# Two-layer streaming encoder on one core: the three cheap steps of each up-projection block moved from places 2, 4 and 5 to places 1, 3 and 5

## The chip, the cores and the metric

The kernel runs on one core of a Trainium2 chip. The metric is the device time of one execution in microseconds (us), lower being better. Three runs of the kernel before are shown, and one further execution was recorded by the profiler.

In the profile, PE is the matrix engine's matmuls and PEld its weight loads, DVE is the vector engine, ACT the scalar engine, POOL the GpSimd engine, and SP the engine whose queue issues the loads.

## The reference, cut to what matters

The input is 256 tokens of width 2048. Two layers each mix tokens in three groups of attention heads, project back, and then apply a multilayer perceptron (MLP) with 8192 hidden columns. All numbers are float32. The part that the change touches is the second line of the MLP:

```
h = rms_norm(x, mlp_norm[l])
u = h @ w_up[l]                      # (256 x 2048) @ (2048 x 8192)
x = x + square(relu(u)) @ w_down[l]  # (256 x 8192) @ (8192 x 2048)
```

## The kernel before, in words

**Blocks.** In each layer the MLP walks over four quarters of the hidden columns (`qt`). A quarter is two up-projection blocks and then two down-projection blocks, each one an instance of `Product`. In names a block is `u` or `d`, the quarter, and 0 or 1: `u10` and `u11` are the up blocks of quarter 1, and `u?0` below stands for the first block of any quarter. There are 16 up blocks and 16 down blocks. A block multiplies 256 rows by 1024 columns and sums over eight *steps* `i` = 0 to 7 of 256 each (line 321, `step`). Weights of a step are two halves of 128x1024, 512 KB each.

**A float32 product from three matmuls.** A weight half arrives in a `raw` tile. ACT copies its head into `wh` (line 154) and DVE subtracts to get the rest, `wl` (line 155). The activations were split in the same way. Each block product is then three matmuls, head by head, head by rest and rest by head (line 313, `add`).

**Plain steps and steps with sums.** A step is a 2x2 by 2x2 product of blocks. A plain step does all eight block products, 24 matmuls of 512 columns. The steps in a list (`S_UP` for up blocks, `S_DOWN` for down blocks, line 278) do it with seven block products of sums and differences, 21 matmuls. For that, DVE forms four combinations of the weights in place (lines 345 to 348), ACT and DVE split those into `th` and `tl`, and the combinations of the activations (`sums`) are made once per layer, while the output projection's results are added to x (lines 801 to 803). In such a step the matmuls come in the order p1, p2, p3 (nine matmuls from `wh` and `wl`), p5, p7, p6, p4 (twelve from `th` and `tl`).

**Buffers.** `raw` has 4 buffers and `wh` and `wl` have 5 each, in all of the kernel. A step with sums loads its halves into `rs`, of which there are 3, and its combinations go to `th` and `tl`, of which there are 2 each. A step with sums takes two of the three `rs` buffers: half 0 holds b11 and b21, half 1 holds b12 and b22. `th_2`/`tl_2` are made from half 1 and come first, `th_3`/`tl_3` from half 0. After `tl_2` half 1's buffer is free, after `tl_3` half 0's.

**What hangs on a block's end.** At the last step with sums (place 5 before and after the change, line 361) DVE begins to combine the accumulators (lines 365 to 369), and at the block's end it adds the rest (line 375). An up block's result gets its ReLU on ACT (line 819), is turned by transposes on PE (line 384), squared on ACT and split on ACT and DVE (`hidden`, four calls). These four calls wait in a list, and `more()` takes one after each pair of block products of a plain step, so all four run in step 0 of the block that follows.

**Order.** A scheduler puts the instructions of each engine into one fixed order when the kernel is built; each engine runs its own list in that order, and waits for others by semaphores. All the weight loads are issued from SP's list, so that a load that waits for a free buffer holds up the loads that stand behind it.

Of the kernel before, what the change touches and what calls it, by code (L numbers as in the profile page):

```python
# [36 lines left out]
def hybrid_encoder(ctx: ExitStack, tc: tile.TileContext, xT, wA, wQ, wKV, wB, wC, wO, wU, wD,  # L37
# [237 lines left out]

    S_UP, S_DOWN = (2, 4, 5), (2, 5)
    HALF = (slice(0, P), slice(P, T))

    later = []
# [688 lines left out]
def build(shapes):  # L970
    import concourse.bacc as bacc

    nc = bacc.Bacc("TRN2", target_bir_lowering=False, num_devices=1)
    args = [nc.dram_tensor(f"in_{n}_dram", shapes[n], F32, kind="ExternalInput").ap() for n in _ORDER]
    args.append(nc.dram_tensor("out_0_dram", (T, D), F32, kind="ExternalOutput").ap())
    with tile.TileContext(nc) as tc:
        hybrid_encoder(tc, *args)
    return nc
# [9 lines left out]
```

## Time and profile before

| | us |
|---|---|
| median of 3 runs (lowest, highest) | 2089.03 (2084.41, 2090.4) |
| the profiled execution, and its span | 2083.71, 2081.9 |
| DVE busy | 1710.9 (82%) |
| ACT busy | 1191.1 (57%) |
| POOL busy | 184.1 (9%) |
| PE busy | 2030.8 (98%) |

Busy time is the time in which an engine executed instructions. PE's clock was granted nearly in full (0.994 on average over the span). The second quarter of the first layer's MLP, as an example, has its two up blocks from 507.44 to 595.60 us of the span and its two down blocks from there to 682.15 us. An engine other than PE matters here only where PE stood and waited for it.

### The profile page before, as it was taken

The numbers are of one execution on the slowest core, as the hardware profiler recorded it, in microseconds if no ns is written. First come the engines' busy times: TensorE is split into PE (matmuls) and PEld (weight loads), VectorE is DVE, ScalarE is ACT, GpSimd is POOL, SyncE is SP. The second block draws the span as 40 slices with busy tenths as digits, with TensorE's granted clock in tenths as the row PEclk, the third lists the DMA queues.
The fourth block names the chain that finished last, engine by engine and source line by source line (L and its number), as shares of the span: only waits on it lengthen the run. The fifth ranks groups of instructions, "written<-read, shape, count | busy, mean of one in ns | idle before, by whom it ended". The sixth has DMA issues, their size and how long they took to land.

```text
span 2081.9 us, 27549 instructions
## 1 busy us (share of the span) xinstructions
PE 2030.8 (98%) x9984; PEld 1694.1 (81%) x9984; DVE 1710.9 (82%) x2427; ACT 1191.1 (57%) x1721; POOL 184.1 (9%) x241
## 2 busy tenths in 40 slices
PE   8999999999999999999999999999999999999997
PEld 6888888888778778878788888877887787787886
DVE  7766697888888888789976766978888988988986
ACT  6666655554664565465566666546546645645663
POOL 5101141000000000000231012400000000000000
PEclk9999999999999999999999999999999999999999
DMA  7534454555556546556445345545555555465562
GB/s 255 191 125 173 148 201 160 189 207 183 181 193 221 188 167 205 180 179 216 161 160 180 130 157 177 194 173 186 179 189 181 205 210 172 172 212 199 195 212 92
DMA packets 106840, 379.92 MB, mean 182 GB/s; under 512 B 11984, under 2 KB 13392, under 8 KB 106704
## 3 DMA queue, kind: packets, MB, share of 16 engines
q1 hardware_dynamic: 104976, 374.85, 51.8%
q10 hardware_dynamic: 1296, 1.62, 0.3%
q8 instruction: 78, 1.28, 0.2%
q0 software_dynamic: 432, 1.70, 0.2%
q14 instruction: 58, 0.48, 0.1%
HBM read 376.03 MB, written 2.10 MB: 182 GB/s over the span
## 4 chain that ended last, share of the span: by engine, by line
PE 68%; DVE 13%; DMA 9%; issue 5%; ACT 4%; POOL 1%; SPq 0%; ACTq 0%; POOLq 0%; DVEq 0%
PE p_d L313 23%; PE p_u L313 8%; PE e_d L313 6%; DMA rs_u<-in_wU_dram 6%; PE ps_wo L164 4%; DVE wl_u L155 3%; DVE tl_u L155 3%; PE ps_wo L165 2%; ACT wh_u L154 2%; PE e_u L313 2%; PE ps_qC L164 1%; PE ps_kC L164 1%; PE ps_kB L164 1%; PE ps_qB L164 1%; DMA raw_d<-in_wD_dram 1%
## 5 line engine op out<-in xcount | busy, mean ns | idle before, releaser
L313 PE MATMUL p_d<-wh_d,h_u 128*128 128x512 f32 x1280 | 420.6, 392 | 0.0
L313 PE MATMUL p_u<-wh_u,xm 128*128 128x512 f32 x1152 | 386.7, 394 | 0.0
L154 ACT CAST wh_d<-raw_d 128x1024 fp32r<-128x1024 f32 x192 | 201.0, 1053 | 195.1 <-PE e_d L313 61.7
L313 PEld LDWEIGHTS p_d<-wh_d,h_u 128*128 128x128 f32 x1280 | 240.1, 188 | 49.4
L313 PEld LDWEIGHTS p_u<-wh_u,xm 128*128 128x128 f32 x1152 | 218.1, 189 | 45.5
L155 DVE TENSOR_TENSOR wl_d<-raw_d,wh_d 128x1024 fp32r<-128x1024 f32 x192 | 232.7, 1221 | 24.5 <-ACT wh_d L154 23.9
L313 PE MATMUL p_d<-wl_d,h_u 128*128 128x512 f32 x640 | 249.4, 390 | 0.0
L154 ACT CAST wh_u<-raw_u 128x1024 fp32r<-128x1024 f32 x160 | 164.8, 1049 | 120.0 <-PE p_u L313 49.4
L313 PE MATMUL p_u<-wl_u,xm 128*128 128x512 f32 x576 | 226.1, 392 | 0.0
L155 DVE TENSOR_TENSOR wl_u<-raw_u,wh_u 128x1024 fp32r<-128x1024 f32 x160 | 193.0, 1218 | 11.5 <-ACT wh_u L154 10.6
L154 ACT CAST wh_u<-rs_u 128x1024 fp32r<-128x1024 f32 x96 | 80.4, 837 | 138.6 <-DMA rs_u<-in_wU_dram 82.4
L155 DVE TENSOR_TENSOR wl_u<-rs_u,wh_u 128x1024 fp32r<-128x1024 f32 x96 | 90.9, 956 | 71.5 <-ACT wh_u L154 70.0
L313 PEld LDWEIGHTS p_d<-wl_d,h_u 128*128 128x128 f32 x640 | 120.5, 188 | 24.3
L313 PE MATMUL e_d<-wh_d,h_u 128*128 128x512 f32 x384 | 134.7, 391 | 0.0
L154 ACT CAST th_u<-rs_u 128x1024 fp32r<-128x1024 f32 x96 | 100.1, 1049 | 49.1 <-DVE rs_u L348 24.2
L313 PEld LDWEIGHTS p_u<-wl_u,xm 128*128 128x128 f32 x576 | 109.4, 190 | 22.3
L155 DVE TENSOR_TENSOR tl_u<-rs_u,th_u 128x1024 fp32r<-128x1024 f32 x96 | 116.4, 1218 | 10.0 <-ACT th_u L154 9.5
L313 PE MATMUL p_u<-th_u,s_xm 128*128 128x512 f32 x288 | 103.1, 403 | 13.7 <-ACT th_u L154 13.7
L313 PE MATMUL e_u<-wh_u,xm 128*128 128x512 f32 x320 | 112.4, 392 | 0.0
L155 DVE TENSOR_TENSOR wl_d<-rs_d,wh_d 128x1024 fp32r<-128x1024 f32 x64 | 62.7, 980 | 52.0 <-ACT wh_d L154 52.0
L154 ACT CAST wh_d<-rs_d 128x1024 fp32r<-128x1024 f32 x64 | 53.4, 834 | 91.0 <-PE p_d L313 71.4
L140 DVE TENSOR_TENSOR wl_wo<-raw_wo,wh_wo 128x1024 fp32r<-128x1024 f32 x64 | 85.4, 1335 | 20.1 <-ACT wh_wo L139 19.6
(464 smaller groups left out, 4766.1 us busy)
## 6 DMA issues: line engine op xcount, KB each, us to landing
raw_d<-in_wD_dram SPq DMA_DIRECT2D x192, 512.0 KB, 5.2
raw_u<-in_wU_dram SPq DMA_DIRECT2D x160, 512.0 KB, 4.6
rs_u<-in_wU_dram SPq DMA_DIRECT2D x96, 512.0 KB, 4.0
raw_wo<-in_wO_dram SPq DMA_DIRECT2D x64, 512.0 KB, 3.7
rs_d<-in_wD_dram SPq DMA_DIRECT2D x64, 512.0 KB, 4.8
raw_qB<-in_wB_dram SPq DMA_DIRECT2D x16, 512.0 KB, 4.3
raw_kB<-in_wB_dram SPq DMA_DIRECT2D x16, 512.0 KB, 4.0
raw_vB<-in_wB_dram SPq DMA_DIRECT2D x16, 512.0 KB, 4.3
```

What stands on the lines that cost most here:

```text
L140: nc.vector.tensor_tensor(wl[:, :n], raw[:, :n], as32(wh[:, :n]), op=ALU.subtract)
L154: nc.scalar.copy(h, src)
L155: (eng or nc.vector).tensor_tensor(l, src, as32(h), op=ALU.subtract)
L164: nc.tensor.matmul(ps, wh, a, start=i == 0, stop=False)
L165: nc.tensor.matmul(ps[:, 1, :], wl, a[:, 0, :], start=False, stop=i == n - 1)
L313: nc.tensor.matmul(self.ps[b], x, y, start=self.n[b] == 1, stop=self.n[b] == self.total[b])
```

## The change

One table of places is changed. Step 5 keeps its sums; the sums of step 2 go to step 1 and those of step 4 go to step 3. The number of plain steps and of steps with sums stays the same in every block, and so does every operation's count and size. The down blocks are not changed.

```
-    S_UP, S_DOWN = (2, 4, 5), (2, 5)
+    S_UP, S_DOWN = (1, 3, 5), (2, 5)
```

What the scheduler makes of it is seen at three places. Names have the block, the layer, the step and the half or combination: `rs_u10_0_5_1` is block u10 in layer 0, step 5, half 1.

The first is SP's list of loads for block u10. Before:

```order
L328 DMA raw_u10_0_6_0_5425<-in_wU_dram 128x1024
L328 DMA raw_u10_0_6_1_5426<-in_wU_dram 128x1024
L328 DMA raw_u10_0_7_0_5461<-in_wU_dram 128x1024
L328 DMA rs_u10_0_4_1_5329<-in_wU_dram 128x1024
L328 DMA rs_u10_0_5_0_5373<-in_wU_dram 128x1024
L328 DMA raw_u10_0_7_1_5462<-in_wU_dram 128x1024
L328 DMA rs_u10_0_5_1_5374<-in_wU_dram 128x1024
```

The same place in SP's list after the change:

```order
L328 DMA raw_u10_0_6_0_5425<-in_wU_dram 128x1024
L328 DMA rs_u10_0_3_1_5293<-in_wU_dram 128x1024
L328 DMA raw_u10_0_6_1_5426<-in_wU_dram 128x1024
L328 DMA rs_u10_0_5_0_5373<-in_wU_dram 128x1024
L328 DMA raw_u10_0_7_0_5461<-in_wU_dram 128x1024
L328 DMA rs_u10_0_5_1_5374<-in_wU_dram 128x1024
```

The second half of the middle step with sums now stands two loads earlier, and the second half of step 5 has a plain step's time more between it and the one before.

The second place is DVE's list at the start of block u11, where the four `hidden` calls of u10 run (`h0` to `h3` and `sf_h2` are theirs, and line 375 ends u10). Before, from the last line 375 on:

```order
L375 TENSOR_TENSOR c1_u10_0_5419<-e_u10_0_5200,c1_u10_0_5419 128x512
L155 TENSOR_TENSOR wl_u11_0_2_0_5634<-rs_u11_0_2_0_5629,wh_u11_0_2_0_5633 128x1024
L155 TENSOR_TENSOR h0_u10_0_5527<-a0_u10_0_5525,h0_u10_0_5527 128x2x256
L155 TENSOR_TENSOR wl_u11_0_2_1_5645<-rs_u11_0_2_1_5630,wh_u11_0_2_1_5644 128x512
L345 TENSOR_TENSOR rs_u11_0_2_1_5630<-rs_u11_0_2_1_5630 128x512
L155 TENSOR_TENSOR h1_u10_0_5544<-a1_u10_0_5542,h1_u10_0_5544 128x2x256
L346 TENSOR_TENSOR rs_u11_0_2_1_5630<-rs_u11_0_2_0_5629,rs_u11_0_2_1_5630 128x512
```

After:

```order
L375 TENSOR_TENSOR c1_u10_0_5419<-e_u10_0_5200,c1_u10_0_5419 128x512
L346 TENSOR_TENSOR rs_u11_0_1_1_5594<-rs_u11_0_1_0_5593,rs_u11_0_1_1_5594 128x512
L155 TENSOR_TENSOR wl_u11_0_2_0_5647<-raw_u11_0_2_0_5642,wh_u11_0_2_0_5646 128x1024
L347 TENSOR_TENSOR rs_u11_0_1_0_5593<-rs_u11_0_1_1_5594,rs_u11_0_1_0_5593 128x512
L155 TENSOR_TENSOR tl_u11_0_1_2_5620<-rs_u11_0_1_1_5594,th_u11_0_1_2_5619 128x1024
L155 TENSOR_TENSOR h0_u10_0_5527<-a0_u10_0_5525,h0_u10_0_5527 128x2x256
L348 TENSOR_TENSOR rs_u11_0_1_0_5593<-rs_u11_0_1_0_5593 128x512
L155 TENSOR_TENSOR wl_u11_0_2_1_5663<-raw_u11_0_2_1_5643,wh_u11_0_2_1_5662 128x1024
L155 TENSOR_TENSOR h1_u10_0_5544<-a1_u10_0_5542,h1_u10_0_5544 128x2x256
L293 TENSOR_TENSOR sf_h2_u10_0_5568<-a2_u10_0_5563 128x128 x2
L293 TENSOR_TENSOR sf_h2_u10_0_5568<-sf_h2_u10_0_5568,a2_u10_0_5563 128x128
L155 TENSOR_TENSOR tl_u11_0_1_3_5632<-rs_u11_0_1_0_5593,th_u11_0_1_3_5631 128x1024
```

The first step with sums of u11 is now prepared among the work that the end of u10 leaves, and its `tl` come ahead of `h2` and `h3`. Behind these rows DVE's list goes on with h2, one sf, wl of step 3's halves, s_h2, h3, line 345 of step 3, wl of step 4's half 0, lines 346 to 348, wl of step 4's half 1, and then step 3's two `tl`.

The third place is DVE's list at the start of the first layer's MLP (line 781 adds the output projection's last result to x, in two parts). After the change:

```order
L345 TENSOR_TENSOR rs_u00_0_1_1_3778<-rs_u00_0_1_1_3778 128x512
L346 TENSOR_TENSOR rs_u00_0_1_1_3778<-rs_u00_0_1_0_3777,rs_u00_0_1_1_3778 128x512
L347 TENSOR_TENSOR rs_u00_0_1_0_3777<-rs_u00_0_1_1_3778,rs_u00_0_1_0_3777 128x512
L781 TENSOR_TENSOR x7_in_80<-ps_wo15_0_3671,x7_in_80 128x256
L348 TENSOR_TENSOR rs_u00_0_1_0_3777<-rs_u00_0_1_0_3777 128x512
L781 TENSOR_TENSOR x7_in_80<-ps_wo15_0_3671,x7_in_80 128x256
```

Before, the two parts of line 781 stood together, ahead of all four combinations.

## Rows read from the trace of the kernel before

**Rows 1.** The page's first section: busy us (share of the span) xinstructions.

```profile
span 2081.9 us, 27549 instructions
PE 2030.8 (98%) x9984; PEld 1694.1 (81%) x9984; DVE 1710.9 (82%) x2427; ACT 1191.1 (57%) x1721; POOL 184.1 (9%) x241
```

**Rows 2.** Waits of PE: who waited for whom, us in total, times, longest us.

```profile
PE p_u L313 <- ACT th_u L154: 13.7, 16, 1.6
PE p_u L313 <- DVE tl_u L155: 6.9, 8, 1.2
```

**Rows 3.** Timeline of PE, block u10: start, us, what, count, [idle before <-releaser].

```profile
530.79 0.39 PE L313 MATMUL p_u<-tl_u,s_xm 128*128 128x512 f32 x1
...
535.10 0.39 PE L313 MATMUL p_u<-wh_u,s_xm 128*128 128x512 f32 x1
536.16 0.73 PE L313 MATMUL p_u<-th_u,s_xm 128*128 128x512 f32 x2 [0.68 <-ACT th_u L154]
536.73 0.40 PE L313 MATMUL p_u<-wh_u,xm 128*128 128x512 f32 x1
537.88 0.50 PE L313 MATMUL p_u<-tl_u,s_xm 128*128 128x512 f32 x1 [0.75 <-DVE tl_u L155]
538.21 0.39 PE L313 MATMUL p_u<-th_u,s_xm 128*128 128x512 f32 x1
```

**Rows 4.** The chain that ended last, 500 to 600 us: start us, us, what.

```profile
516.91 4.79 DMA rs_u<-in_wU_dram
...
527.50 3.56 DMA rs_u<-in_wU_dram
```

**Rows 5.** Timeline of DVE, block u10.

```profile
515.66 2.35 DVE L155 TENSOR_TENSOR tl_u<-rs_u,th_u 128x1024 fp32r<-128x1024 f32 x2
...
526.26 1.22 DVE L155 TENSOR_TENSOR tl_u<-rs_u,th_u 128x1024 fp32r<-128x1024 f32 x1
...
536.61 1.21 DVE L155 TENSOR_TENSOR tl_u<-rs_u,th_u 128x1024 fp32r<-128x1024 f32 x1
```

**Rows 6.** Timeline of ACT, end of block d01 (the cast is u10's, step 2, half 0).

```profile
507.64 1.06 ACT L154 CAST wh_u<-rs_u 128x1024 fp32r<-128x1024 f32 x1 [1.66 <-PE e_d L313]
```

**Rows 7.** Timeline of PE: u11's first matmuls and step 5, last up block's step 5.

```profile
550.96 0.39 PE L313 MATMUL p_u<-wh_u,xm 128*128 128x512 f32 x1
...
552.32 0.60 PE L384 MATMUL t_u<-ident,c_u 128*128 128x128 f32 x4
552.67 0.48 PE L313 MATMUL p_u<-wh_u,xm 128*128 128x512 f32 x1
552.99 0.40 PE L313 MATMUL p_u<-wl_u,xm 128*128 128x512 f32 x1
...
582.01 0.73 PE L313 MATMUL p_u<-th_u,s_xm 128*128 128x512 f32 x2 [0.68 <-ACT th_u L154]
...
1969.29 0.73 PE L313 MATMUL p_u<-th_u,s_xm 128*128 128x512 f32 x2 [0.52 <-ACT th_u L154]
```

**Rows 8.** Timeline of DVE, block u11, from the last line 375 of u10 on.

```profile
551.31 0.68 DVE L375 TENSOR_TENSOR c_u<-e_u,c_u 128x512 f32<-128x512 f32 x1
552.28 1.23 DVE L155 TENSOR_TENSOR wl_u<-rs_u,wh_u 128x1024 fp32r<-128x1024 f32 x1 [0.30 <-ACT wh_u L154]
554.65 0.69 DVE L155 TENSOR_TENSOR h_u<-a_u,h_u 128x512 fp32r<-128x512 f32 x1 [1.15 <-ACT h_u L154]
...
557.19 0.68 DVE L346 TENSOR_TENSOR rs_u<-rs_u,rs_u 128x512 f32<-128x512 f32 x1
557.79 0.48 DVE L293 TENSOR_TENSOR sf_h_u<-a_u 128x128 f32<-128x128 f32 x2
558.20 0.68 DVE L155 TENSOR_TENSOR h_u<-a_u,h_u 128x512 fp32r<-128x512 f32 x1
```

**Rows 9.** Busy us (x instructions) of each engine in blocks u10 and u11.

```profile
507.44:551.30 43.86, 42.43 (x186) 34.49 (x185) 37.39 (x43) 23.05 (x26) 0.00 (x0) 1.00 0.53 187
551.30:595.60 44.30, 43.62 (x199) 35.33 (x198) 39.07 (x51) 28.55 (x36) 0.00 (x0) 1.00 0.53 185
```

## The prediction, made before the changed kernel was run

> **What bounds the kernel now.** I read the page's head first. PE is busy for 2030.8 of 2081.9 us [rows 1], so the change can only earn what PE loses in waiting. The view of PE's waits says where that is: 16 waits for `th_u` and 8 for `tl_u`, 20.6 us in all [rows 2], every one of them in an up block. In PE's timeline all 24 stand in step 5, the second of the two neighbouring steps with sums. A first block of a quarter (u?0) has two, as in [rows 3]; a second block (u?1) has one of 0.52 to 0.68 us, the 0.68 in u11 and the 0.52 in the last of the eight [rows 7]. The eight of u?1 add to 4.8 us, so the sixteen of u?0 hold 15.8.
>
> A wait costs more than its idle time. From 530.79 to 535.10 PE starts 19 matmuls, one every 0.227 us [rows 3], though one lasts 0.39, since they overlap. From 535.10 to 536.16 it starts one, which loses 0.83 where 0.68 is called idle; the next two take 0.57 instead of 0.45. The wait behind it loses 0.92 and 0.10 where 0.75 is idle. So each wait loses about 0.27 us on top.
>
> Why step 5 is late is read from the chain and from DVE's timeline. The chain goes through two loads of `rs`, each of which starts within 0.03 us of the end of a `tl` [rows 4, 5]: there are three `rs` buffers, so the second half of the next step with sums waits until the step before it has made `tl_2`. In u10 step 4's `tl_2` ends at 526.26 + 1.22 = 527.48, the load takes 3.56, and cast, subtraction, combinations and `tl_2` of step 5 follow until 536.61 + 1.21 = 537.82. This loop takes 10.34 us. From step 2 to step 4 it took 10.60 (515.66 + 1.22 = 516.88 to 527.48).
>
> PE needs far less between two neighbours: 21 matmuls of 0.227, 4.77 us. Step 4's `tl_2` came 3.31 us before its use at 530.79, so step 5's is late by 10.34 - 4.77 - 3.31 = 2.26. PE's record says 2.32: due at 530.79 + 4.77 = 535.56, used at 537.88 [rows 3]. With a plain step between, PE has 45 matmuls, 10.2 us, to the loop's 10.3 to 10.6.
>
> **The change in the first blocks, u?0.** Nothing is added or removed; each step carries its instructions and its two loads to another place. The question is only whether step 1 is ready in time, since 3 and 5 follow from it. Block u10 starts at 507.44 [rows 9]; the first `tl` of step 1 is its eleventh matmul, due at 507.44 + 24 x 0.227 + 10 x 0.227 = 515.2. On the supply side, the cast of step 2's first half began at 507.64, when PE's last `e_d` matmul had freed a `wh` buffer [rows 6], and its `tl_2` ended at 516.88. One step earlier in the rotation of those buffers is 5.45 us earlier, so 511.4. The four additions of line 375 now fall into this stretch as well, at 0.60 us each (the distance from 557.19 to 557.79 [rows 8]); if they all delay it, 513.8. Step 1 has 1.4 to 3.8 us to spare. Each loop of 10.34 to 10.60 against 10.2 takes 0.1 to 0.4 of that, twice, so step 5 still has at least 0.6. SP's list does not spoil this: ahead of the second half of step 3 stands only a load whose `raw` buffer is free once `wl` of step 2's half 0 is made, and DVE makes that before step 1's `tl_2`. The two waits in each of eight blocks go: 15.8 + 16 x 0.27 = **20.1 us**.
>
> **The second blocks, u?1.** Here step 0 also carries the four `hidden` calls, and step 1 now lies right behind it. I count along DVE's new list from the last line 375, at 551.31 [rows 8]: up to step 1's `tl_3` stand six operations of 512 columns at 0.60, four of 1024 at 1.13 (the pair in [rows 5] takes 2.35, one alone 1.22) and three small ones at 0.20, 8.7 us. That is 560.0 if DVE never waits, and 561.5 with the 0.30 and 1.15 us that it idled there before [rows 8]. PE starts the block at 550.96; a group of transposes takes 0.35 and 0.09 in the matmul behind it [rows 7], four of them 1.76; `tl_3` is used after 24 + 16 matmuls: 550.96 + 1.76 + 9.08 = 561.8. So 0.3 to 1.8 us are left.
>
> From there to step 3's `tl_2` are eight operations of 512, four of 1024 and a small one, 9.5 us: 569.5 to 571.0, due at 570.6. Step 5 follows by the loop: 579.9 to 581.4, due at 580.8. Its `tl_3` stands behind line 348 and two `wl` (4.0 us): 583.9 to 585.4, due 14 matmuls later at 584.0. Delays don't add up, as a stall also moves what is due later. So a second block loses between 0 and 1.3 us plus up to three restarts of 0.27, 0 to 2.1 us; before it lost 0.60 + 0.27 = 0.87. I take about that again, the middle of the bounds: **0**, with -7 to +10 us for all eight.
>
> **The start of the MLP.** The two additions of line 781 now come behind three and four combinations, at most 4 x 0.60 = 2.4 us later [rows 8]. PE's matmul on the last squares (line 213) waits for them, but PE's new list puts six matmuls of the block, 1.36 us, ahead of it. That leaves 0 to 1, and some more if ACT, which now has two casts of `th` ahead of that square, is later: 0 to 2 us, of which I take 0.7, in two layers **+1.4 us**. The sums of the activations, made a little earlier in the output projection, are the same operations, and in that stage PE's view of waits has no entry; PE's matmuls cover them, and they cost about 2 us of DVE's time a layer (two operations of 512 and four small ones) if that cover is gone.
>
> **The sum.** -20.1 + 0 + 1.4 = -18.7 us, against the profiled execution's 2083.71: 2065.0. The three runs and that execution average 2086.9, 3.2 us above it, so I forecast **2068**.
>
> **Rivals.** *The second blocks lose their waits too* (the lower bounds): -20.1 - 7 + 1.4, about 2061. DVE idles 11.7 us in the pair of blocks (88.16 less 37.39 and 39.07 [rows 9]), which speaks for it; the order in its list, against it.
>
> *The wait moves instead of going*: in u?1 step 1 stands in the busiest part of DVE and ACT. If the casts of `th`, now among ReLU and squares on ACT, come 2 us later than I count, each second block loses some 2.5 us more than before, 20 in all: about 2088, no change. It decides from about 1.7 us beyond the margin. ACT's 28.55 of 44.30 us busy in u11 [rows 9] speak against it.
>
> *DVE's operations do not overlap at all.* If each took its whole 0.68 or 1.22 us before the next could start, the 27 operations up to step 3's second `tl` in u?1 would take about 2 us more, and the second blocks would give back some 16 us: about 2084, no change. Against it stand the starts at 557.19 and 557.79, 0.60 apart, for an operation that lasts 0.68 [rows 8]. The Trainium skill, "VectorE: DVE Perf Modes", section "The DRAIN you can't avoid", says that the next operation does not start until the pipe is empty; the rows here show starts before the end, and I go by the rows.
>
> *Slower*: `tl_3` of step 1 stands behind `h1` in DVE's fixed list. `h1` hangs on the block's last additions, ReLU, transposes and squares, and holds up everything behind it, the free `rs` buffer and step 3 included. DVE already waited 1.15 us for such an `h` [rows 8]. Beyond the 1.8 us at most to spare, each further us costs one in each of eight blocks. It outweighs the gain from about 2.3 us on; with 3.2, about 2094.
>
> **Chances.** The forecast with its own range of 2062 to 2080: 0.65. Second blocks free as well: 0.15. The wait moves: 0.12. No overlap on DVE: 0.03. Slower: 0.05. The measurement of this kernel tells about 0.3%, 6 us, from no change. The case without overlap, at 2084, lies within it or just short, and I count it as no change: faster 0.80, same 0.15, slower 0.05. For the range I leave out the slower case and about half of the moved wait, and below a tenth of the best case: 2057 to 2085.
>
> **What would show it.** Right: PE's waits for `th_u` and `tl_u` in the first blocks are gone; u10's 43.86 us fall to about 41.9; the time from one `tl_2` to the next with sums is still about 10.3 us, now with a plain step between; what is left stands in the second blocks, under about 1 us each. Wrong: waits of 2 us or more in steps 1 or 3 of the second blocks, with DVE standing before an `h` or a `tl`; new waits of PE before a `p1` because a load is late; or u10 as long as before.

## The result, and the profile after

| | before | after |
|---|---|---|
| median, us (lowest to highest, 4 runs each) | 2086.74 (2084.41 to 2090.4) | 2063.23 (2059.76 to 2065.67) |
| profiled execution, its span | 2083.71, 2081.9 | 2064.82, 2063.0 |

The ratio is 0.9885, with a 95% interval of 0.986 to 0.9909: the change makes the kernel 1.1% faster. The span is 18.9 us shorter.

The head of the page after the change answers to [rows 1]: as many matmuls, 8.3 us less of PE's busy time.

```profile
span 2063.0 us, 27559 instructions
PE 2022.5 (98%) x9984; PEld 1691.4 (82%) x9984; DVE 1708.3 (83%) x2427; ACT 1182.0 (57%) x1721; POOL 186.1 (9%) x241
```

The view of PE's waits after the change, to be read beside [rows 2] (who waited for whom, us in total, times, longest us):

```profile
PE p_u L313 <- DVE tl_u L155: 9.9, 16, 1.2
...
PE t_u L384 <- ACT a_u L824: 1.0, 3, 0.4
...
PE e_u L313 <- ACT a_u L824: 0.5, 1, 0.5
PE p_u L313 <- ACT th_u L154: 0.2, 1, 0.2
```

Of 20.6 us of waiting for `th_u` and `tl_u`, 10.1 are left. In PE's timeline all 16 waits for `tl_u` stand in step 5 of a second block, two in each; no first block has one.

Where the time went is seen best by blocks. Each length runs in PE's timeline from a block's first matmul to the first of the next (in us; each cell lists the four quarters in their order; [rows 9] end u10 at 551.30, the table at u11's first matmul, 550.96 [rows 7]):

| | first blocks u?0, layer 0 | layer 1 | sum | second blocks u?1, layer 0 | layer 1 | sum |
|---|---|---|---|---|---|---|
| before | 45.25 43.52 44.26 45.69 | 47.22 45.98 46.05 44.13 | 362.1 | 44.58 44.64 44.50 44.47 | 44.63 44.58 44.62 44.48 | 356.5 |
| after | 43.42 41.48 41.49 41.48 | 43.44 41.49 41.49 41.49 | 335.8 | 46.25 47.68 45.56 45.12 | 45.56 46.07 46.35 45.56 | 368.2 |

The first blocks gave 26.3 us and the second blocks took back 11.7. The pairs of down blocks gave another 4.0, and the rest of the program stayed as it was to 0.3. 26.3 - 11.7 + 4.0 = 18.6, against 18.9 in the span.

The windows of u10, u11 and u21 after the change (length, then busy us and instructions of PE, PEld, DVE, ACT and POOL, then PE's granted clock, DMA share, GB/s); the first two answer to [rows 9]:

```profile
506.08:547.56 41.48, 41.48 (x185) 34.36 (x183) 34.60 (x40) 21.24 (x24) 0.00 (x0) 1.00 0.60 195
547.56:595.24 47.68, 45.03 (x201) 35.54 (x199) 42.00 (x54) 29.76 (x38) 0.00 (x0) 1.00 0.57 193
...
722.93:768.49 45.56, 44.28 (x200) 35.69 (x199) 39.78 (x51) 28.06 (x36) 0.00 (x0) 1.00 0.59 196
```

In u10 PE is busy for all of the 41.48 us: that block is at its floor. In u11 it lacks 2.65, in u21 1.28.

**What a second block waits for now.** PE's timeline of u21, step 5, after the change (start, us, what, count, [idle before <-releaser]):

```profile
752.69 0.39 PE L313 MATMUL p_u<-th_u,s_xm 128*128 128x512 f32 x1
754.13 0.50 PE L313 MATMUL p_u<-tl_u,s_xm 128*128 128x512 f32 x1 [1.05 <-DVE tl_u L155]
754.47 0.63 PE L313 MATMUL p_u<-th_u,s_xm 128*128 128x512 f32 x2
...
757.31 0.61 PE L313 MATMUL p_u<-wh_u,xm 128*128 128x512 f32 x2
758.14 0.50 PE L313 MATMUL p_u<-tl_u,s_xm 128*128 128x512 f32 x1 [0.21 <-DVE tl_u L155]
```

The chain that ended last, in the same stretch (start, us, what), shows why `tl` is late:

```profile
741.80 5.49 DMA rs_u<-in_wU_dram
...
747.39 0.63 ACT wh_u L154
...
748.04 0.70 DVE wl_u L155
```

DVE's timeline there shows both ends of the loop:

```profile
740.56 2.35 DVE L155 TENSOR_TENSOR tl_u<-rs_u,th_u 128x1024 fp32r<-128x1024 f32 x2
...
748.04 0.69 DVE L155 TENSOR_TENSOR wl_u<-rs_u,wh_u 128x512 fp32r<-128x512 f32 x1 [4.00 <-ACT wh_u L154]
748.77 0.69 DVE L345 TENSOR_TENSOR rs_u<-rs_u 128x512 f32<-128x512 f32 x1
749.38 1.22 DVE L155 TENSOR_TENSOR wl_u<-raw_u,wh_u 128x1024 fp32r<-128x1024 f32 x1
750.51 0.68 DVE L346 TENSOR_TENSOR rs_u<-rs_u,rs_u 128x512 f32<-128x512 f32 x1
751.12 1.22 DVE L155 TENSOR_TENSOR wl_u<-raw_u,wh_u 128x1024 fp32r<-128x1024 f32 x1
752.25 0.68 DVE L347 TENSOR_TENSOR rs_u<-rs_u,rs_u 128x512 f32<-128x512 f32 x1
752.86 1.22 DVE L155 TENSOR_TENSOR tl_u<-rs_u,th_u 128x1024 fp32r<-128x1024 f32 x1
```

Step 3's `tl_2` is the first of the pair at 740.56, and the load that waited for its buffer starts at 741.80. Step 5's `tl_2` ends at 752.86 + 1.22 = 754.08, and PE takes it at 754.13. The loop is 754.08 - 741.80 = 12.3 us, where [rows 4, 5] had 10.3 to 10.6. The whole difference to the 10.34 of the two neighbours is the load, which takes 5.49 instead of 3.56. What follows the load takes 6.8 us in both: two `wl` of a plain step stand between the combinations here (749.38 and 751.12), and two stood there in before's loop, in DVE's timeline of u10:

```profile
533.13 1.22 DVE L155 TENSOR_TENSOR wl_u<-raw_u,wh_u 128x1024 fp32r<-128x1024 f32 x1
...
534.87 1.22 DVE L155 TENSOR_TENSOR wl_u<-raw_u,wh_u 128x1024 fp32r<-128x1024 f32 x1
```

In all eight second blocks this loop takes 11.8 to 12.7 us, with loads of 4.9 to 5.9. SP's timeline after the change shows what went out around the load of 5.49:

```profile
740.67 0.33 SPq L328 DMA_DIRECT2D raw_u<-in_wU_dram  x1
741.80 0.33 SPq L328 DMA_DIRECT2D rs_u<-in_wU_dram  x1
742.94 0.33 SPq L328 DMA_DIRECT2D rs_d<-in_wD_dram  x1
```

A plain load went out 1.13 us ahead of it and another half of a step 1.14 us behind it. Ahead of the load of 3.56 us in [rows 4], at 527.50, the last load had gone out at 519.18, and the next followed 3 us later.

**Why the first blocks gave more than their waits.** The granted clock has a part in it, as is seen in the trace of before, in PE's timeline of the first block of the first layer's last quarter:

```profile
887.37 0.73 PE L313 MATMUL p_u<-th_u,s_xm 128*128 128x512 f32 x2 [1.38 <-ACT th_u L154]
887.94 0.40 PE L313 MATMUL p_u<-wh_u,xm 128*128 128x512 f32 x1
889.08 0.80 PE L313 MATMUL p_u<-tl_u,s_xm 128*128 128x512 f32 x1 [0.75 <-DVE tl_u L155]
889.68 0.63 PE L313 MATMUL p_u<-th_u,s_xm 128*128 128x512 f32 x1
890.10 0.63 PE L313 MATMUL p_u<-tl_u,s_xm 128*128 128x512 f32 x1
890.53 0.63 PE L313 MATMUL p_u<-th_u,s_xm 128*128 128x512 f32 x1
```

Windows of before over this place and over step 5 of u10:

```profile
889.00:892.00 3.00, 2.92 (x7) 2.34 (x8) 3.00 (x5) 1.82 (x2) 0.00 (x0) 0.50 0.80 285
...
536.00:540.00 4.00, 3.09 (x12) 2.27 (x13) 4.00 (x6) 3.55 (x5) 0.00 (x0) 1.00 0.84 285
```

Behind the two waits the granted clock is 0.50, which is the 1.2 GHz level, for about 3 us; matmuls start 0.42 to 0.43 us apart instead of 0.227. In u10, with waits of 0.68 and 0.75, it stays at 1.00. Windows over the other first blocks of before show the same fall in three of them (0.63 to 0.66 over 4 to 4.8 us, at 1393, 1570 and 1748 us), so in four of eight. Those four lie 4.21, 3.78, 4.50 and 4.57 us above the length that they have after the change, 17.1 in all; the four without a fall 1.84, 2.04, 2.78 and 2.65, 9.3 in all. After the change no first block has a wait, and the granted clock is 1.00 in all of the up blocks. How many falls an execution of before has differs: over its 20 runs beside the experiments the mean granted clock goes from 0.997 (2077.65 us) to 0.991 (2091.5 us). The 26.3 us are those of the profiled execution, at 0.994.

### The profile page after: what moved, and what is told of

It is laid out like the page before. It is cut to its first block, busy times and chain, and to the rows that moved or that the text cites. A ratio compares the mean times of both kernels' runs of the same rounds, so it can differ in the third digit from the quotient of the medians.

```text
span 2063.0 us, 27559 instructions
## 1 busy us (share of the span) xinstructions
PE 2022.5 (98%) x9984; PEld 1691.4 (82%) x9984; DVE 1708.3 (83%) x2427; ACT 1182.0 (57%) x1721; POOL 186.1 (9%) x241
## 3 DMA queue, kind: packets, MB, share of 16 engines
q8 instruction: 78, 1.28, 0.3%
## 4 chain that ended last, share of the span: by engine, by line
PE 73%; DVE 13%; DMA 6%; issue 6%; ACT 1%; POOL 1%; SPq 0%; DVEq 0%; POOLq 0%; ACTq 0%
PE p_d L313 24%; PE p_u L313 11%; PE e_d L313 6%; DVE wl_u L155 5%; PE ps_wo L164 4%; DMA rs_u<-in_wU_dram 4%; PE e_u L313 3%; PE ps_wo L165 2%; DVE tl_u L155 2%; PE ps_qC L164 1%; PE ps_kB L164 1%; PE ps_kC L164 1%; PE ps_qB L164 1%; DVE rs_u L346 1%; DVE rs_u L347 1%
```

## The experiments

The theory behind the forecast: a step with sums is late because its second half waits for one of three `rs` buffers and must then be loaded, cast and combined (the loop). Neighbours leave PE too little work to cover that, a plain step between nearly enough. The rival: the buffers matter little, and neighbours cost time since DVE makes two steps' parts in one go. Before measured 2084.59 us as the median of 7 runs beside the first four kernels and of 13 beside the last three.

### Four buffers, places of before

```
-    S_UP, S_DOWN = (1, 3, 5), (2, 5)
+    S_UP, S_DOWN = (2, 4, 5), (2, 5)
-    ... tag="u", name=name, bufs=24)
+    ... tag="u", name=name, bufs=23)
-    ... tag="rs", name=f"rs_{nm}_{c}", bufs=3)
+    ... tag="rs", name=f"rs_{nm}_{c}", bufs=4)
```

> The places before the change (2, 4, 5), with four buffers for the halves of steps with sums instead of three (room for it from one of 24 activation buffers, which moves nothing in the MLP's lists). Theory of the load: step 5 was late because its second half could not be loaded until step 4 had made its first tl. With four buffers it loads early, the wait of PE in step 5 goes, first blocks fall from 45.3 us on average to about 41.5 to 42.5 and the whole to about 2055. Rival, the work: two neighbouring steps ask about 13 us of DVE in 9.5 us of PE, so step 5 is late whatever the load does; first blocks stay above 44 us and the whole at 2080 or more.

Measured: 2064.15 us (one run). The waits for `th_u` are gone. 14 waits for `tl_u` are left, 14.9 us in all and up to 2.6 us each in step 5 of a first block. The first blocks sum to 350.3 us, the second blocks to 351.9. What makes `tl_u` late without the wait for a buffer stands in this kernel's DVE timeline, u10:

```profile
530.77 0.69 DVE L347 TENSOR_TENSOR rs_u<-rs_u,rs_u 128x512 f32<-128x512 f32 x1
531.38 1.22 DVE L155 TENSOR_TENSOR wl_u<-raw_u,wh_u 128x1024 fp32r<-128x1024 f32 x1
532.51 0.68 DVE L348 TENSOR_TENSOR rs_u<-rs_u 128x512 f32<-128x512 f32 x1
533.12 2.35 DVE L155 TENSOR_TENSOR wl_u<-raw_u,wh_u 128x1024 fp32r<-128x1024 f32 x2
535.39 2.35 DVE L155 TENSOR_TENSOR tl_u<-rs_u,th_u 128x1024 fp32r<-128x1024 f32 x2
```

DVE does not stand still here; three `wl` of plain steps are ahead of the two `tl` in its fixed list, where before's list has two ahead of the first `tl`. So each theory has a part: the buffer gives about 20 us, and some 1.8 us a first block (350.3 against 335.8 after the change) stay with the neighbours and DVE's order.

### Four buffers, places of after

This is the changed kernel with the last two lines of the diff above (23 and 4).

> The changed places (1, 3, 5) with four such buffers. Theory of the load: what second blocks still lose in step 5 (46.0 us on average, against 43.3 without any wait) is the same wait for a buffer, with a load that took 5.5 us; with four buffers second blocks fall to 43.3 to 44 us and the whole from 2063 to about 2045. Rival, DVE's backlog from the hidden calls: the loads are early but the subtractions are not; second blocks stay above 45 us and the whole within 5 us of 2063.

Measured: 2042.25 us (2041.87 to 2042.92, 4 runs), ratio 0.9803 (0.9784 to 0.9822). The first blocks sum to 335.8 us as after the change, the second blocks to 346.9, 43.36 each. PE waits for nothing in any up block; the wait of the MLP that is left is

```profile
PE p_d L313 <- DVE tl_d L155: 2.7, 1, 2.7
```

which before had too. The second blocks' 368.2 - 346.9 = 21.3 us are the whole difference to the changed kernel's 2063.23. What these blocks lost after the change came from the buffer, and the theory of the load holds here. Part of the gain is DVE's list, which the scheduler made anew: in u21 the loop from step 3's `tl_2` to step 5's takes 7.9 us instead of 12.3, and about 1.1 of these 4.4 us are a `wl` of a plain step that no longer stands in it. This is the fastest of the versions shown.

### One place more between the second and third step with sums

```
-    S_UP, S_DOWN = (1, 3, 5), (2, 5)
+    S_UP, S_DOWN = (1, 3, 6), (2, 5)
```

> Places 1, 3 and 6, three buffers. Theory of the load: from step 3 to step 6 PE has 69 matmuls, 15.7 us, which is more than the loop of 10.3 to 12.3 us, so the wait in the last step with sums goes from second blocks (46.0 to 43.3 to 44 us). The block's end is the price: the accumulators are combined one step later, and the transposes in the next block may wait 0 to 1.5 us. Whole 2045 to 2063. Rival, DVE's backlog: DVE is short of time in second blocks wherever the steps lie, and the end is tighter too; whole 2063 or more.

Measured: 2044.91 us (2043.56 to 2046.43), ratio 0.9814 (0.979 to 0.9837). Three buffers do nearly as well as four, with two plain steps to cover the last loop: no waits for `th_u` or `tl_u`, first blocks 41.48 us (43.9 in u00), second blocks 43.6. Again as the theory of the load has it.

### Neighbours at the start of a block

```
-    S_UP, S_DOWN = (1, 3, 5), (2, 5)
+    S_UP, S_DOWN = (1, 2, 5), (2, 5)
```

> Places 1, 2 and 5: neighbours again, but at the front, with step 5 standing alone. Theory of the load: step 2 now gets 21 matmuls, 4.8 us, for a loop of 10.3 us, and step 1 had 1.4 to 3.8 us to spare, so PE waits 2 to 4 us in step 2 of first blocks (43.5 to 46 us each) and no longer in step 5; whole 2080 to 2100. Rival: the wait belonged to step 5, close to the block's end, and not to neighbours; then first blocks are near 41.5 us and the whole near 2060.

Measured: 2049.62 us (one run), faster than the changed kernel: the expectation was missed. The loop is as long as ever, from a `tl_2` that ends at 679.40 in u20 to one that ends at 689.31, 9.9 us, and PE's due time for it does come earlier. But PE's timeline of u20 shows no wait in that step:

```profile
687.05 0.39 PE L313 MATMUL p_u<-wh_u,s_xm 128*128 128x512 f32 x1
687.27 0.39 PE L313 MATMUL p_u<-wh_u,xm 128*128 128x512 f32 x1
687.65 0.73 PE L313 MATMUL p_u<-th_u,s_xm 128*128 128x512 f32 x2
688.21 0.40 PE L313 MATMUL p_u<-wl_u,xm 128*128 128x512 f32 x1
...
689.14 0.62 PE L313 MATMUL p_u<-wh_u,xm 128*128 128x512 f32 x2
689.59 0.39 PE L313 MATMUL p_u<-tl_u,s_xm 128*128 128x512 f32 x1
```

Between the last matmul from `wh_u,s_xm` and the first from `tl_u` this block runs matmuls from `wh_u,xm` and `wl_u,xm`: they are step 3's, which the scheduler put there. One stands ahead of step 2's first two with `th` and six behind them; in before's u10 there is one of step 6 in that place ([rows 3], 536.73). So a late step costs only what PE's fixed list doesn't fill, which the expectation left out. One of the eight first blocks does wait for `th_u` in step 2, 1.38 us at 1532.31, and two second blocks wait for ACT's squares, 0.85 and 0.75 us.

### Only the first of the three moved

```
-    S_UP, S_DOWN = (2, 4, 5), (2, 5)
+    S_UP, S_DOWN = (1, 4, 5), (2, 5)
```

> Sums at places 1, 4 and 5, three rs buffers: only the first of the three is moved from the places of before, and the two neighbours at the end stay. Theory of the loop and its margin: what counts is how early the step ahead was. With two plain steps between 1 and 4 (about 15.3 us of PE) against a loop of 10.4 to 12.3 us, step 4 has 3 to 5 us more to spare than the 3.3 us of before, and the loop from 4 to 5 (10.3 us) against PE's 4.8 is then covered or nearly so: waits of the first blocks under 0.5 us, the total 2042 to 2052. In PE's list five matmuls of step 6 instead of one now stand between step 5's first matmul with th and the first with tl, which covers 0.9 us more of a late tl. Theory of neighbours: two neighbouring steps of sums at a block's end cost the wait for th wherever the third stands, some 0.7 us idle and 0.27 restart a block and the clock's fall with it: first blocks stay at 44 us or more, the total 2065 to 2085.

Measured: 2057.99 us (2057.38 to 2058.23, 4 runs), ratio 0.9877 (0.9845 to 0.9909): between the two expectations. Every up block waits once, for `th_u` alone, 0.17 to 0.63 us:

```profile
PE p_u L313 <- ACT th_u L154: 5.1, 16, 0.6
```

The filling was foreseen rightly: the wait for `tl_u` is covered by five matmuls of step 6. The margin was not. Step 4 was to be 3 to 5 us earlier than in before; its `tl_2` ends at 524.24, and PE first uses it at 527.89: 3.65 us to spare, 0.3 more than the 3.31 of before. ACT's timeline of this kernel says why:

```profile
517.71 0.62 ACT L154 CAST wh_u<-rs_u 128x512 fp32r<-128x512 f32 x1 [4.11 <-PE p_u L313]
```

The cast of step 4's second half waited 4.11 us for PE, which had to free one of the five `wh` buffers. The step can't be made earlier however early its loads are, as [rows 6] showed for step 2.

### Only the second of the three moved

```
-    S_UP, S_DOWN = (2, 4, 5), (2, 5)
+    S_UP, S_DOWN = (2, 3, 5), (2, 5)
```

> Sums at places 2, 3 and 5, three rs buffers: only the middle step is moved from the places of before. Theory of the loop and its margin: the pair is now 2 and 3, and step 2 stands where it stood before, with perhaps 3 us to spare, so step 3 is late by 2 us in the first blocks as step 5 was before; PE's list has no matmul of step 4 between step 3's p3 and its first with th, and five of step 4 before the first with tl, so the wait for th of 0.7 us remains and that for tl is covered. Step 5 then has one plain step between and a loop of 10.4 to 12.3 us against 10.2: little wait. First blocks at 42.5 to 44 us, the total 2055 to 2072. If the loads' buffer were no part of it and only the place at a block's end cost time, this kernel would have no waits: about 2044.

Measured: 2084.94 us (2083.32 to 2088.91, 10 runs), ratio 1.0003 (0.9988 to 1.0018): no change, and outside what the theory of the loop gave (2055 to 2072). That the place at a block's end alone costs the time (2044) is ruled out. The wait at the pair came as expected, but step 5 waits as well, in PE's timeline of u10:

```profile
526.82 0.73 PE L313 MATMUL p_u<-th_u,s_xm 128*128 128x512 f32 x2 [0.61 <-ACT th_u L154]
538.97 0.73 PE L313 MATMUL p_u<-th_u,s_xm 128*128 128x512 f32 x2 [1.10 <-ACT th_u L154]
542.45 0.50 PE L313 MATMUL p_u<-tl_u,s_xm 128*128 128x512 f32 x1 [0.24 <-DVE tl_u L155]
```

The load in the chain between the two takes 5.38 us, from 528.51; a plain load had gone out 1.7 us ahead of it. In DVE's list three `wl` of plain steps, from 535.97, 537.71 and 539.44, stand in the loop instead of two, and it takes 13.9 us. With a margin of nothing left at step 3, the longer loop shows in full. The first blocks sum to 357.6 us and the second to 368.4.

### Two buffers, places of after

```
-    ... tag="rs", name=f"rs_{nm}_{c}", bufs=3)
+    ... tag="rs", name=f"rs_{nm}_{c}", bufs=2)
```

> The changed places 1, 3 and 5 with two rs buffers instead of three, the other direction of the test with four. Theory of the load: both halves of the next step now wait, one for tl_2 and one for tl_3, some 1.2 to 4 us later, so the loop grows to 13.5 to 16 us against PE's 10.2 with a plain step between; every up block, the first ones too, waits 2 to 5 us in step 3 and again in step 5: 16 blocks by 5 to 10 us, the total 2130 to 2200. If the loop were set by DVE's own list and not by the buffers, the blocks would stay as they are with three: about 2063.

Measured: 2125.44 us (2 runs, 2123.4 and 2127.47), ratio 1.0201 (1.0156 to 1.0245). Slower, as the theory of the load has it, though a little less than its range. The first blocks sum to 357.5 us, the second to 390.5, and PE now waits for plain steps too:

```profile
PE p_u L313 <- DVE tl_u L155: 10.0, 16, 1.2
PE p_u L313 <- DVE wl_u L155: 8.1, 21, 0.6
PE p_u L313 <- ACT wh_u L154: 7.2, 17, 0.7
PE p_u L313 <- ACT th_u L154: 6.9, 10, 1.0
```

With two, three and four buffers at the same places the time is 2125, 2063 and 2042 us.

## Why the prediction was right, and where its terms were off

The forecast was 2068 with a range of 2057 to 2085, and 2063.23 was measured. The main step held: with the neighbours parted, step 5 of the first blocks is ready in time and its waits are gone. The total is nearer than its terms, two of which were off in opposite directions; that the sum came out at -18.7 and the span at -18.9 us is luck.

**First blocks, -20.1 forecast, -26.3 measured.** All 16 waits are gone, and step 1 is ready in time, as worked out: in u10 its `tl_2` has 3.3 us to spare, where 1.4 to 3.8 were forecast. The term was under-sized because a wait was priced at its idle time and 0.27 us of restart. In the four blocks of before where the clock held, that is right: 2.51 us a block were priced and 2.33 found (9.3 over four). In the other four the granted clock stood at 0.50 behind the two waits, and a block lost 4.3 us. The rows for that stood in before's trace; the argument had looked at u10, where it doesn't happen.

**Second blocks, 0 forecast, bounds -7 to +10, +11.7 measured.** This step failed, and just outside its bounds. The count along DVE's list up to step 3 held: its `tl_2` was to end 18.5 to 20.0 us after the block's first matmul (569.5 to 571.0 less 550.96), and in u21 it ended 741.78 - 722.93 = 18.9 after it. Seven of the eight blocks lie within, from 18.9 to 19.9; u11 has 21.0. "Step 5 follows by the loop" was wrong: the loop was taken as 10.34 us, that of two neighbours, while in u21 it is 12.3, all of it in a load of 5.49 us instead of 3.56. [rows 4, 5] had a hint in the load of 4.79 us from step 2 to step 4, and before's trace had more: from step 2 to step 4, with a plain step between, the loop took 10.6 to 11.9 us in the 16 up blocks, and u10's 10.60 was the shortest. In the first blocks after the change the last load had gone out 3.2 to 3.9 us ahead of that `rs` load, and the loop took 10.0 to 10.9 us in seven of them; in u10 it took 12.2, which the 2.65 us that step 3 had to spare covered. In u11 2 us more were lost where PE waited for ACT's squares, 0.38, 0.49 and 0.32 idle at 553 to 556 us.

**Start of the MLP, +1.4 forecast.** 0 measured: after the change u00, in which that matmul stands, is 43.42 us long and PE is busy for all of it, so the matmuls ahead covered the two additions; the stretch between the layers takes 412.9 us in both traces.

**Down blocks, not in the sum, -4.0 measured.** Before had four waits of PE's transposes for ReLU at the start of a down pair, 2.8 us idle, which are gone. With them the pairs had taken 86.3 to 87.5 us; now they take 86.2. Why ReLU was late there stays open. Step 5's delay alone does not do it: the changed kernel and the one with places 2, 3 and 5 wait up to 1.2 us in step 5 of their second blocks, where before waits 0.5 to 0.7, and they have none of these waits.

**The rivals.** The wait moved in part: 11.7 us came back in the second blocks, but in step 5, where the rival had put it in step 1 and at 20 us. The one with `tl_3` behind `h1` did not occur; step 3 was in time. The one without overlap on DVE didn't either: after the change the operations at 748.77 and 749.38 start 0.61 apart with 0.69 us for the first, and the second does not use its result. The forecast took only half of what the Trainium skill, "VectorE: DVE Perf Modes", section "The DRAIN you can't avoid", says: the section adds that a next operation which is not held starts earlier. These starts agree with that half.

**Open.** That a load is slow because another went out shortly ahead of it is read from rows, and no run moved a plain load alone; in u10 after the change one took 5.69 us though the last had gone out 3.2 us ahead. Why the clock falls behind two waits in four blocks of before and not in the others was not tested. The size of the waits does not tell them apart: 1.42 and 0.75 us in u20 of the first layer left it at 1.00, 0.64 and 1.22 us in u00 of the second did not. With places 2, 3 and 5, u10 has three waits, and its clock stays at 1.00 all the same. Behind the one wait of a down block for `tl_d`, 2.6 to 2.7 us, the clock falls after the change (0.83 over 1000 to 1010 us) and does not with four buffers and the same places.

## What to carry to other kernels

A loop of "buffer free, load, cast, combine" should be timed in the surroundings that the change gives it: the same loop took 10.3 us between neighbours, 12.3 where another load had gone out 1.1 us ahead of its own, and 13.9 where one more `wl` of another step stood in it as well. One more buffer in that loop was worth as much as the whole reordering, so when one gap comes back at the same step of every block, try the buffers before the order; the Trainium skill, "Perfetto Trace Analysis", section "Optimization Strategy", reads a gap that repeats as a possible lack of room for the next tile, and the runs with two, three and four buffers agree (2125, 2063, 2042 us). How early a step is can be capped elsewhere, here by PE freeing `wh`, and a late one costs only what the waiting engine's fixed list doesn't fill.

## What the runs showed of the hardware that was not expected

Two short waits of PE, 1.38 and 0.75 us with three matmuls between, were followed by a granted clock of 0.50 for about 3 us in a kernel whose clock is 0.994 on average; in four of the eight blocks with two waits this cost nearly as much again (4.3 us a block instead of 2.3). The `rs` loads of 512 KB inside the two MLPs, over all nine traces, took 3.1 to 4.5 us (82 loads, median 3.5) when none had gone out for 8 us or more, and 3.8 to 7.9 us (381 loads, median 5.6) when another of the same size had gone out 1.0 to 1.3 us ahead.
